# Hybrid decoder layer on eight cores: sums of squares moved from TensorE to POOL, adaLN slots kept between projection pieces, and the last attention head interleaved with the output projection

## The chip, the cores and the metric

The kernel runs on all 8 cores of one Trainium2 chip. Each core computes one of eight sequences, and the cores do not communicate. The metric is the device time of the slowest core, in microseconds (us). Executions of this program have a second, slower state, in which some cores show a lower granted TensorE clock; those executions are left out wherever two kernels are compared. Stage times below are medians over the 8 cores of one profiled execution, so a stage time does not depend on which core happened to be the slowest.

The engines are PE (TensorE), DVE (VectorE), ACT (ScalarE), POOL (GpSimd) and SP (which only issues DMA here).

## The reference, cut to what matters

`x` is (8, 2048, 2048) in float32. The layer is (cut and shortened):

```python
mod = silu(c) @ w_mod + b_mod                  # (B, 6*2048): shift, scale, gate, twice ("adaLN")
h = rmsnorm(x, g_pre_mix) * (1 + sc_a) + sh_a
fq, fk, fv, fg, sq, sk, sv = split(h @ w_in)
fox = forgetting_attention(fq, fk, fv, log_sigmoid(fg + b_forget))   # "FoX": 8 heads, causal, decay bias
swa = sliding_window_sink_attention(rope(sq), rope(sk), sv, sinks)   # 8 heads, window 128
mix = concat(fox, swa) @ w_out
x = x + gt_a * rmsnorm(mix, g_post_mix)
h = rmsnorm(x, g_pre_mlp) * (1 + sc_m) + sh_m
y = square(relu(h @ w_up)) @ w_down            # d_ff = 8192
x = x + gt_m * rmsnorm(y, g_post_mlp)
```

`rmsnorm` needs the sum of squares over the model width for every token. The kernel keeps the width on the 128 partitions and in 16 rows, and 512 tokens along the free axis. A sum over the width is thus a sum over 16 rows and over the partitions.

## The kernel before

The order of the work is: two of the six parts of `mod` with the first projections; FoX heads 0 and 1; sliding window; FoX heads 2 to 7; four tiles of `w_out` (512 tokens each); then up, down, up, down for two halves of the tokens; then a tail with the last residual.

**The filler.** Attention leaves gaps on PE. Between its steps a filler lays pieces of projections for later heads (`main`: 4 matmuls of 128x512 count as 4), and after every 8th piece a *slot* of the other four parts of `mod` (`side`). One slot is four small matmuls on one 1 MB-in-fp32 tile of `w_mod`, which a ring of five buffers loads as 512 KB of bf16.

```python
def _one(self):
    while self.main:
        ...                              # next piece; StopIteration removes it
        self.n += 1
        if self.n % self.every == 0:     # every = 8
            self._side()
        return v
    return self._side()                  # no pieces left: run slots alone

def fill(self, n):
    self.credit += n
    while self.credit > 0:
        v = self._one()
        if v is None:
            self.credit = 0
            return
        self.credit -= v
...
F.main = [q_(1), k_(1), stripe(I_SK, sk_ev(0)), vpair(I_SV, vts)] + [...4 stripes]
fox(0, 64 * 6 + 128 + 64 + 18)           # the second argument is the budget of filling
F.main = [...]
fox(1, 64 * 7 + 128 + 18)
...                                      # sliding window, FoX 2 to 6: 128 + 4 each
F.drain_side()
for m in range(16):
    dma("pool", WO[m](), dram(T["wO"][m]), f"wo{m}")
fox(7, 0, sbanks=[2, 3, 0, 1], la=3)     # last head: nothing to fill with
```

The last slot of each of the four parts is followed by `mod_finish`: DVE copies the result to `stage`, and PE, DVE turn it into a column of `modT`. In the memory layout of before, `stage` shares its 2 KB with `rr`, which every FoX head uses.

**Attention.** A score matmul goes to a bank; DVE subtracts the decay row (`cfb`, loaded by DMA from `crow`), ACT takes the exponential into one of four buffers `Pb`, and PE multiplies `Pb` with V and with ones.

**Sums of squares** after `w_out`, and after `down`, are made on PE: ACT squares each row into a bf16 buffer and PE adds it up over the partitions by a matmul with ones, 16 for one sum.

```python
def stat_add(src, sbk, first, last):
    flush(1)
    q = sqb[cnt["q"] % 2]
    cnt["q"] += 1
    act(q(), src, AF.Square)                       # bf16
    pend.append(lambda: pe([mm(sbk(), ones(), q(), first, last)], ...))

def rstd_of(bk):
    flush(0)
    act(bk(), bk(), AF.Ln, bias=EPS, scale=1.0 / D)
    act(bk(), bk(), AF.Exp, scale=-0.5)
```

While PE computes tile t of `w_out`, the other engines do the two norms of tile t-1 as a list of 35 jobs. Two jobs follow each of the first nine rows and three each of the other seven:

```python
jobs = [lambda: rstd_of(sb1)]                      # norm 1
jobs += [lambda m=m: p1(m) for m in range(KC)]     # y*gate*rstd + x, and its square
jobs += [lambda: rstd_of(sb2)]                     # norm 2 needs all 16 squares of p1
jobs += [lambda m=m: p2(m) for m in range(KC)]     # input of the MLP
if t + 1 < NT:
    jobs += [lambda: x2_load(t + 1)]
```

The softmax here doesn't subtract the row's maximum and nothing guards it: scores larger than these inputs give would overflow.

## Time and profile before

The time before was 3306.3 us (median of 3 runs, 3305.73 to 3306.89).

These lines are from the page of the kernel before: busy time of each engine with its share of the span; three rows of the 40 slices of the span (tenths of busy time, of the full TensorE clock, and of the DMA engines); and the shares of the chain of work that ended last.

```profile
PE 2930.7 (89%) x14392; PEld 1371.9 (41%) x14392; DVE 877.6 (27%) x1343; ACT 754.9 (23%) x1228; POOL 358.5 (11%) x502
...
PE   2278957969888889999999999999999999999994
...
PEclk9988978979999999999999999999999999999997
DMA  9834566460111352336444455555689744444446
...
PE 79%; DMA 7%; DVE 4%; ACT 4%; issue 4%; POOL 2%; DVEq 0%; ACTq 0%; POOLq 0%; SPq 0%
```

The reader should see two things. PE is the limit nearly everywhere, from slice 10 on at 80% or more until the tail. And in slices 6 and 9 (counted from 1) PE falls to 5 and 6 tenths and the clock to 7 tenths, while DMA goes up to 6. The 7% of DMA in the chain must be there.

This is the table of windows for the kernel before: each line is a stretch (start:end, its length), the busy time of each engine, the granted clock, the DMA share and GB/s.

```profile
core 5: us, PE busy (x) PEld busy (x) DVE busy (x) ACT busy (x) POOL busy (x), PEclk, DMA share, GB/s
454.00:509.50 55.50, 13.90 (x95) 5.42 (x93) 3.89 (x8) 2.41 (x4) 11.41 (x20) 0.52 0.94 148
683.00:721.50 38.50, 8.45 (x59) 3.12 (x51) 1.85 (x3) 1.23 (x2) 7.40 (x14) 0.57 1.02 161
721.50:841.00 119.50, 117.30 (x763) 71.13 (x763) 48.60 (x74) 71.83 (x130) 2.11 (x4) 0.98 0.14 25
1156.00:1198.00 42.00, 27.93 (x135) 12.49 (x132) 25.79 (x45) 27.13 (x48) 0.53 (x1) 0.88 0.67 131
1256.40:1470.20 213.80, 192.80 (x865) 83.03 (x863) 131.74 (x192) 96.28 (x156) 0.00 (x0) 0.99 0.31 119
```

The first two stretches, at the ends of FoX 0 and FoX 1, hold 94 us in which PE works 22 us, at about half the clock, and the DMA engines are full. The sliding window (third line) has nearly no DMA (0.14). The fourth line is FoX 7, the fifth is tiles 1 to 3 of `w_out`.

PE's timeline in the first of these stretches shows what PE does there. The columns are start, duration, engine, line, operation, operands, count, and in brackets the idle time before it with what ended that.

```profile
466.71 0.62 PE L379 MATMUL bank<-ring_67,condpad 128*32 128x512 bf16 x4 [4.75 <-DMA ring_67<-w_mod]
470.30 0.62 PE L379 MATMUL bank<-ring_71,condpad 128*32 128x512 bf16 x4 [2.98 <-DMA ring_71<-w_mod]
473.60 0.62 PE L379 MATMUL bank<-ring_68,condpad 128*32 128x512 bf16 x4 [2.69 <-DMA ring_68<-w_mod]
```

Each slot is 0.6 us of work behind 2.7 to 4.8 us of waiting for its tile. Those are the slots that the filler runs when its pieces are used up.

### The profile page before, as it was taken

The numbers are of one execution on the slowest core, as the hardware profiler recorded it, in microseconds if no ns is written. First come the engines' busy times: TensorE is split into PE (matmuls) and PEld (weight loads), VectorE is DVE, ScalarE is ACT, GpSimd is POOL, SyncE is SP. The second block draws the span as 40 slices with busy tenths as digits, with TensorE's granted clock in tenths as the row PEclk, the third lists the DMA queues.
The fourth block names the chain that finished last, engine by engine and source line by source line (L and its number), as shares of the span: only waits on it lengthen the run. The fifth ranks groups of instructions, "written<-read, shape, count | busy, mean of one in ns | idle before, by whom it ended". The sixth has DMA issues, their size and how long they took to land.

```text
span 3307.3 us, 37215 instructions; the slowest of 8 cores (3281.3 to 3307.3 us)
## 1 busy us (share of the span) xinstructions
PE 2930.7 (89%) x14392; PEld 1371.9 (41%) x14392; DVE 877.6 (27%) x1343; ACT 754.9 (23%) x1228; POOL 358.5 (11%) x502
## 2 busy tenths in 40 slices
PE   2278957969888889999999999999999999999994
PEld 0034523436533434334444444444444444444441
DVE  0132323314444445554211100000033311000005
ACT  1141323316445444443211100000111111000000
POOL 1341222210000100000000000000000000000003
PEclk9988978979999999999999999999999999999997
DMA  9834566460111352336444455555689744444446
GB/s 185 154 103 98 87 111 113 85 113 14 29 41 25 61 134 90 115 109 123 76 76 76 77 89 95 92 91 92 127 170 189 143 77 77 77 76 73 75 84 215
DMA packets 99197, 325.71 MB, mean 98 GB/s; under 512 B 12080, under 2 KB 12208, under 8 KB 92624
## 3 DMA queue, kind: packets, MB, share of 16 engines
q0 software_dynamic: 58320, 211.87, 39.4%
q1 hardware_dynamic: 40704, 111.46, 10.0%
q8 instruction: 117, 1.92, 0.2%
q14 instruction: 56, 0.46, 0.1%
HBM read 493.12 MB, written 42.01 MB: 162 GB/s over the span
## 4 chain that ended last, share of the span: by engine, by line
PE 79%; DMA 7%; DVE 4%; ACT 4%; issue 4%; POOL 2%; DVEq 0%; ACTq 0%; POOLq 0%; SPq 0%
PE bank L379 79%; DMA ring_70<-w_mod 5%; DVE bank L399 2%; POOL qrot L399 1%; ACT qrot L396 1%; DMA ring_69<-w_mod 1%; DVE xstA L404 1%; DVE mixF L404 1%; ACT rr L396 1%; ACT sqA L396 1%; DMA xstA<-xP 0%; DMA cfb_83<-crow 0%; ACT Pb_89 L396 0%; DMA cfb_85<-crow 0%; ACT sqb_182 L396 0%
## 5 line engine op out<-in xcount | busy, mean ns | idle before, releaser
L410 DVE TENSOR_SCALAR bank<-bank 128x512 f32<-128x512 f32 x256 | 166.0, 694 | 643.2 <-PE bank L379 643.2
L379 PE MATMUL bank<-mix,rung_110 128*128 128x512 bf16 x1376 | 304.0, 379 | 0.0
L379 PE MATMUL bank<-mix,rung_108 128*128 128x512 bf16 x1376 | 304.0, 379 | 0.0
L379 PE MATMUL bank<-mix,rung_109 128*128 128x512 bf16 x1344 | 296.9, 379 | 0.0
L413 DVE COPY mixF<-bank 128x512 f32<-128x512 f32 x64 | 41.2, 686 | 854.9 <-PE bank L379 854.9
L396 ACT ACTIVATE sqb_181<-bank 128x512 bf16<-128x512 f32 x64 | 38.2, 597 | 890.2 <-DVE mixF L413 852.2
L379 PEld LDWEIGHTS bank<-mix,rung_110 128*128 128x128 bf16 x1376 | 134.7, 98 | 162.3
L379 PEld LDWEIGHTS bank<-mix,rung_108 128*128 128x128 bf16 x1376 | 134.6, 98 | 162.2
L379 PEld LDWEIGHTS bank<-mix,rung_109 128*128 128x128 bf16 x1344 | 131.5, 98 | 158.6
L379 PE MATMUL bank<-hT,ring_68 128*128 128x512 bf16 x640 | 159.7, 384 | 8.8 <-DVE mix L399 5.4
L379 PE MATMUL bank<-hT,ring_69 128*128 128x512 bf16 x512 | 136.2, 406 | 24.4 <-POOL hT L410 16.9
L399 DVE TENSOR_TENSOR bank<-bank,cfb_85 128x512 f32<-128x512 f32 x192 | 117.8, 628 | 119.1 <-PE bank L379 113.6
L399 DVE TENSOR_TENSOR bank<-bank,cfb_83 128x512 f32<-128x512 f32 (+3 forms) x128 | 74.2, 595 | 89.2 <-PE bank L379 77.5
L379 PEld LDWEIGHTS bank<-hT,ring_68 128*128 128x128 bf16 x640 | 61.2, 98 | 79.4 <-issue 16.9
L396 ACT ACTIVATE Pb_87<-bank,Ctok 128x512 bf16<-128x512 f32 x80 | 55.0, 688 | 147.8 <-DVE bank L399 147.7
L379 PEld LDWEIGHTS bank<-hT,ring_69 128*128 128x128 bf16 x512 | 50.3, 103 | 91.0 <-issue 46.7
L379 PE MATMUL bank<-qT_72,kT_73 128*128 128x512 bf16 (+3 forms) x160 | 55.9, 352 | 35.6 <-ACT Pb_87 L396 27.0
L203 POOL DMA_DIRECT2D rung_108<-wU x43 | 22.7, 528 | 584.4 <-PE bank L379 584.4
L399 DVE TENSOR_TENSOR mix<-bank,rr 128x512 bf16<-128x512 f32 x48 | 33.1, 691 | 144.3 <-ACT rr L396 144.3
L396 ACT ACTIVATE Pb_89<-bank,Ctok 128x512 bf16<-128x512 f32 (+1 forms) x80 | 48.2, 602 | 98.5 <-DVE bank L399 98.5
L379 PE MATMUL bank<-qT_74,kT_75 128*128 128x512 bf16 (+3 forms) x160 | 56.8, 360 | 14.5 <-ACT Pb_87 L396 9.1
L379 PE MATMUL bank<-ring_71,hT 128*128 128x256 bf16 x512 | 67.3, 275 | 1.9 <-DVE skT L399 1.9
(672 smaller groups left out, 4547.8 us busy)
## 6 DMA issues: line engine op xcount, KB each, us to landing
rung_108<-wU POOLq DMA_DIRECT2D x43, 512.0 KB, 5.2
rung_110<-wU POOLq DMA_DIRECT2D x43, 512.0 KB, 5.2
rung_109<-wD POOLq DMA_DIRECT2D x43, 512.0 KB, 5.1
rung_108<-wD POOLq DMA_DIRECT2D x43, 512.0 KB, 5.2
rung_109<-wU POOLq DMA_DIRECT2D x42, 512.0 KB, 5.2
rung_110<-wD POOLq DMA_DIRECT2D x42, 512.0 KB, 5.2
outP<-mixF SPq DMA_DIRECT2D x64, 256.0 KB, 3.1
ring_67<-w_mod POOLq DMA_DIRECT2D x25, 512.0 KB, 8.6
```

The source lines that it names most:

```text
L203: return self.op(eng, lambda e: e.dma_start(out=oa, in_=ia), [in_], [out], dsem=dsem, extra=extra)
L379: ins = e.matmul(o, lhsT=l, rhs=rh, start=st, stop=sp)
L396: return P.op("act", lambda e: e.activation(out=out.ap, in_=in_.ap, func=func, **kw), r, [out])
L399: return P.op(eng, lambda e: e.tensor_tensor(out=out.ap, in0=a.ap, in1=b.ap, op=op), [a, b], [out])
L404: return P.op("dve", lambda e: e.scalar_tensor_tensor(out=out.ap, in0=a.ap, scalar=sc, in1=b.ap, op0=op0, op1=op1), r, [out])
L410: return P.op(eng, lambda e: e.tensor_scalar(out=out.ap, in0=a.ap, scalar1=sc, scalar2=None, op0=op), r, [out])
L413: return P.op("dve", lambda e: e.tensor_copy(out=out.ap, in_=a.ap), [a], [out])
```

## The change

The intent has three parts and some support:

1. Slots run only between projection pieces, one per 8 pieces, never alone. They then spread into the sliding window and FoX 2 to 6, where DMA has room. The slots must then not share memory with FoX, so `stage` gets room of its own; that, and most of what follows, is paid for by a smaller scratch area for DMA.
2. FoX 7 is interleaved with the first tile of `w_out`.
3. Squares are kept in fp32 and added row by row on POOL; PE does one fp32 matmul with ones per sum.
4. Support: six `Pb` in place of four, four weight buffers for up/down in place of three, two V pairs swapped in order.

The core of the diff, with cuts:

```diff
-BASE = 16640
+SCRATCH = 4096
+BASE = SCRATCH + 256
+NPB = 6
+NRB = 4
@@ Fill._one
-            return self._side()
+            return None
@@ fox(h, prefill, ..., skip=0, drain=True)
+            w = tot / (n - skip) / 2 if i >= skip else 0
-            F.fill(tot / n / 2)
+            F.fill(w)
             pv(L[i])
@@ order of the heads
-    fox(0, 64 * 6 + 128 + 64 + 18)
+    fox(0, 64 * 7 + 128)
-    fox(1, 64 * 7 + 128 + 18)
+    fox(1, 64 * 7 + 128)
     ... (128 + 4 becomes 128 for the sliding window and FoX 2 to 6)
-    fox(7, 0, sbanks=[2, 3, 0, 1], la=3)
@@ sums
-    def stat_add(src, sbk, first, last):
+    def stat_add(src, acc, first):
+        if first:
+            act(acc(), src, AF.Square)
+            return
         q = sqb[cnt["q"] % 2]
         cnt["q"] += 1
         act(q(), src, AF.Square)
-        pend.append(lambda: pe([mm(sbk(), ones(), q(), first, last)], [ones(), q()], [sbk()]))
+        tt(acc(), acc(), q(), ALU.add, eng="pool")
-    def rstd_of(bk):
-        flush(0)
+    def rstd_of(acc):
+        bk = banks[SBK[cnt["s"] % 3]]
+        cnt["s"] += 1
+        pe([mm(bk(), onesF(), acc(), True, True)], [onesF(), acc()], [bk()])
@@ w_out
+    def out_tile(t, acc, nxt):
+        for m in range(KC):
+            bk = nxt()
+            for q in (0, 2, 3, 1):       # head 7 lies in group 1, so that comes last
+                pe([... 4 matmuls ...])
+                yield 4
+            ... two or three norm jobs, the copy, the square
+    F.every = 1000
+    F.main = [out_tile(0, acc, next_pj)]
+    fox(7, 4 * 34, skip=6, drain=False)
+    x2_load(0, [1, 2, 3])
+    R2.start()
+    F.drain()
@@ memory: sq0, sq1, acc0, acc1 (fp32), stage on its own, ... (cut)
```

## The prediction

> **What bounds it now.** TensorE: the page gives PE 2930.7 of 3307.3 us (89%); in the chain of waits 79% is PE, 7% DMA. A table of windows gives the stages: start and first projections 0-262 us; FoX head 0 to 454; **454-509.5: PE busy 13.9 us, DMA share 0.94, clock 0.52**; FoX 1 to 683; **683-721.5: PE busy 8.5, DMA 1.02, clock 0.57**; sliding window to 841; FoX 2-6 to 1156 (62-66 us each); FoX 7 to 1198; w_out tiles to 1470 (58.4, then 71.3 each); up/down 452, 448, 442, down to 3265; tail 42.
>
> **Change by change.**
>
> 1. *adaLN slots.* The bold windows are slots that the filler runs when its projection pieces are used up: PE's timeline shows 4 small matmuls (0.6 us), then 2-5 us until the next w_mod tile lands, about 3.2 us a slot. The changed filler never does this; 28 slots go, one per 8 pieces, into sliding window and FoX 2-6 (DMA share 0.05-0.25); between pieces one takes 0.34 us. 55.5+38.5 us go, and about 6 us at low clock after them; back come 28x0.34, 3 us of drain, and 3 us at the start of FoX 1 (FoX 3 waits 3.25 there). **-83 us.**
>
> 2. *FoX 7 with tile 0.* PE needs 23 us (FoX) + 55.2 (256 matmuls at 0.2157 start to start); now they take 100.4. About 10 us of early waits (cfb rows late among the w_out loads: 2.9 and 5.0) stay, as the first six steps get no filling. **-10 us.**
>
> 3. *Sums of squares.* 192 ones-matmuls go (41.4 us), with PE's 0.7 us waits for sqb. Added: 180 POOL adds of 1.26 us (the qrot multiply, same shape) and 12 fp32 ones-matmuls: "FP8 and Floating Point Precision" of the Trainium skill says true FP32 takes 4 passes, so I estimate 0.9 us.
>  Tiles 1-3: PE needs 55.2+1.8, but the second fp32 matmul stands right behind the last residual add. DVE (two rows of 1.6 us and a 0.78 copy per 3.45 us of PE) is behind by then; a square (0.63) and an add (1.26) follow: PE waits about 8 us. 65 instead of 71.3: **-17 us**. POOL, 3.8 us per 3.45 there, is nearly as late.
>  Up/down: 80 ones-matmuls less, 4 fp32 more, one longer wait: **-14 us**.
>  Tail: four squares pass through POOL in turn, then two fp32 matmuls: **+4 us**.
>  The skill ("GPSIMD Engine Reference", Key points) says POOL contends with DVE operations with two SBUF inputs. This trace agrees: the mixF+aX add takes 1.76 us beside POOL, 0.69 alone. DVE operations beside the new adds have a PSUM operand, so I expect no slowing.
>
> 4. *Fourth weight buffer, six Pb, layout, V pairs swapped.* PE doesn't wait for weights in up/down (busy 100%): **about 0**.
>
> Sum about -124: **3182 us**, range 3152 to 3214. Faster by over 2%: 0.96; within: 0.03; slower: 0.01.
>
> **What would show it.** No stretch near 455-510 and 680-720 with DMA near 1.0 and clock near 0.5; FoX 2-6 1-2 us longer each; FoX 7 + tile 0 about 90 us; tiles 1-3 about 65 each, with one PE wait of 6-10 us at the fp32 matmul on POOL's accumulator; down 435-437; tail 46; POOL busy 225 us more.
>
> **What would make it wrong.** w_mod loads colliding with weight loads at their new places; w_out loads late for FoX 7; POOL's queue holding back squares and banks (tiles over 70 us); dearer fp32 matmuls; a lower granted clock in the denser program.

## The result, and the profile after

The changed kernel took 3195.69 us (median of 4 runs: 3196.94, 3194.45, 3192.54 and one slow, 3336.93); the kernel before took 3306.02 us beside it. The ratio of fast runs is 0.9663 (95% interval 0.9644 to 0.9682). A ratio here is the mean time of one kernel's fast runs over that of the other's of the same rounds, so it is not quite the ratio of the quoted medians. So the change is faster by 3.4%, about 110 us; the prediction was 124 us.

The same lines of the page, after:

```profile
PE 2873.5 (90%) x13961; PEld 1359.6 (43%) x14224; DVE 876.0 (27%) x1344; ACT 757.9 (24%) x1228; POOL 585.2 (18%) x682
...
PE   2278988998888898999999999999999999999994
...
PEclk8578999999999998999999999999999999999997
DMA  9834545522333833354444455555688644444455
...
PE 79%; DVE 5%; issue 5%; DMA 4%; ACT 4%; POOL 3%; DVEq 0%; POOLq 0%; ACTq 0%; SPq 0%
```

The two dips are gone: from slice 5 on PE is at 8 or more tenths until the tail, and DMA is spread out. POOL is busy 226.7 us longer (585.2 - 358.5). The DMA share of the chain falls from 7% to 4%.

The windows after are FoX 1, sliding window, FoX 7 with tile 0, and tiles 1 to 3. The columns are those of before.

```profile
core 0: us, PE busy (x) PEld busy (x) DVE busy (x) ACT busy (x) POOL busy (x), PEclk, DMA share, GB/s
458.90:629.10 170.20, 159.35 (x904) 82.31 (x916) 60.46 (x96) 54.61 (x92) 38.86 (x45) 0.98 0.47 81
629.10:743.70 114.60, 112.75 (x790) 74.33 (x793) 50.10 (x75) 72.33 (x131) 6.33 (x12) 1.00 0.32 56
1072.60:1162.20 89.60, 83.53 (x386) 38.11 (x394) 36.78 (x61) 37.39 (x63) 19.84 (x18) 0.92 0.72 141
1162.20:1364.70 202.50, 178.36 (x765) 79.25 (x780) 130.02 (x192) 98.28 (x156) 112.56 (x90) 0.93 0.33 125
```

FoX 1 now has a mean clock of 0.98 (only its first microseconds are still at half clock). Tiles 1 to 3 take 202.5 us instead of 213.8, but their clock has fallen from 0.99 to 0.93: something makes PE idle long enough to lose its clock. The timeline around the second sum of tile 1's norms shows it, first the other engines and then PE:

```profile
1197.49 0.69 DVE L404 TENSOR_TENSOR Y_108<-bank,Y_109 128x512 f32<-128x512 f32 x1
1198.26 0.60 ACT L401 ACTIVATE sq_186<-bank 128x512 f32<-128x512 f32 x1 [0.59 <-DVE Y_108 L404]
1200.01 0.63 ACT L401 ACTIVATE sq_185<-Y_108 128x512 f32<-128x512 f32 x1 [1.15 <-POOL acc_188 L404]
1200.78 1.26 POOL L404 TENSOR_TENSOR acc_188<-acc_188,sq_185 128x512 f32<-128x512 f32 x1
...
1190.93 3.62 PE L384 MATMUL bank<-mix,WO_59 128*128 128x512 bf16 x16
1202.19 2.04 PE L384 MATMUL bank<-acc_188,onesF 128*128 128x512 f32 x2 [7.64 <-POOL acc_188 L404]
1204.03 4.79 PE L384 MATMUL bank<-mix,WO_60 128*128 128x512 bf16 x15
...
1232.83 1.02 PE L384 MATMUL bank<-acc_187,onesF 128*128 128x512 f32 x2
1233.69 3.62 PE L384 MATMUL bank<-mix,WO_52 128*128 128x512 bf16 x16
...
1269.36 2.05 PE L384 MATMUL bank<-acc_188,onesF 128*128 128x512 f32 x2 [7.88 <-POOL acc_188 L404]
1433.25 2.04 PE L384 MATMUL bank<-acc_188,onesF 128*128 128x512 f32 x2 [5.13 <-POOL acc_188 L404]
```

DVE's last residual add of the tile ends at 1198.2, 3.6 us after PE has run out of work (1190.93 + 3.62). Its square comes 1.8 us later: ACT first squares another row (0.60 us), and then waits 1.15 us for a buffer that POOL still reads. POOL's add ends at 1202.04. Then the fp32 matmul takes twice as long as the one at 1232.83, which had no wait, and the next row of 16 matmuls takes 4.79 us for 15 of them instead of 3.62 us for 16.

The stages, in us (medians over the 8 cores of one profiled execution):

| stage | before | after | difference |
|---|---|---|---|
| start and first projections | 271.1 | 269.7 | -1.4 |
| FoX 0 | 232.0 | 184.6 | -47.4 |
| FoX 1 | 209.8 | 169.9 | -39.9 |
| sliding window | 119.4 | 114.6 | -4.8 |
| FoX 2 to 6 (sum) | 314.2 | 327.8 | +13.6 |
| FoX 7 and tile 0 | 100.2 | 88.3 | -11.9 |
| tiles 1 to 3 (sum) | 213.9 | 201.4 | -12.5 |
| up, down, up, down, with the last sums | 1792.8 | 1786.0 | -6.8 |
| tail | 45.8 | 44.5 | -1.3 |
| span, median core | 3300.0 | 3187.0 | -113.0 |

### The profile page after: what moved, and what is told of

It is laid out like the page before. It is cut to its first block, busy times and chain, and to the rows that moved or that the text cites. A ratio compares the mean times of both kernels' runs of the same rounds, so it can differ in the third digit from the quotient of the medians.

```text
span 3195.4 us, 36955 instructions; the slowest of 8 cores (3178.6 to 3195.4 us)
## 1 busy us (share of the span) xinstructions
PE 2873.5 (90%) x13961; PEld 1359.6 (43%) x14224; DVE 876.0 (27%) x1344; ACT 757.9 (24%) x1228; POOL 585.2 (18%) x682
## 3 DMA queue, kind: packets, MB, share of 16 engines
q0 software_dynamic: 58320, 211.87, 39.9%
## 4 chain that ended last, share of the span: by engine, by line
PE 79%; DVE 5%; issue 5%; DMA 4%; ACT 4%; POOL 3%; DVEq 0%; POOLq 0%; ACTq 0%; SPq 0%
PE bank L384 79%; DMA ring_70<-w_mod 4%; DVE bank L404 2%; POOL qrot L404 1%; ACT qrot L401 1%; POOL acc_188 L404 1%; DVE bank L409 1%; DVE xstA L409 1%; ACT rr L401 1%; ACT sqA L401 1%; DVE mixF L409 1%; DMA cfb_80<-crow 0%; DMA xstA<-xP 0%; POOL hT L415 0%; DVE mix L404 0%
## 5 line engine op out<-in xcount | busy, mean ns | idle before, releaser
L401 ACT ACTIVATE sq_185<-bank 128x512 f32<-128x512 f32 x59 | 35.2, 597 | 827.5 <-DVE mixF L418 792.9
L384 PE MATMUL bank<-hT,ring_71 128*128 128x512 bf16 x566 | 142.7, 382 | 3.1 <-DVE mix L404 2.2
L384 PE MATMUL bank<-hT,ring_69 128*128 128x512 bf16 x436 | 117.5, 406 | 27.7 <-POOL hT L415 17.4
L404 POOL TENSOR_TENSOR acc_187<-acc_187,sq_185 128x512 f32<-128x512 f32 x59 | 74.7, 1266 | 122.4 <-ACT sq_185 L401 122.4
L384 PE MATMUL bank<-hT,ring_68 128*128 128x512 bf16 x312 | 79.0, 388 | 4.3 <-DVE mix L404 3.1
L404 POOL TENSOR_TENSOR acc_188<-acc_188,sq_186 128x512 f32<-128x512 f32 x59 | 74.4, 1262 | 45.2 <-ACT sq_186 L401 43.0
L384 PEld LDWEIGHTS bank<-hT,ring_71 128*128 128x128 bf16 x576 | 54.9, 98 | 63.2 <-issue 7.4
L384 PE MATMUL bank<-qT_72,kT_73 128*128 128x512 bf16 (+3 forms) x151 | 52.7, 349 | 32.3 <-ACT Pb_87 L401 20.0
L384 PEld LDWEIGHTS bank<-hT,ring_69 128*128 128x128 bf16 x448 | 43.9, 102 | 85.4 <-issue 46.6
L404 POOL TENSOR_TENSOR qrot<-qrot,sinT 128x512 f32<-128x512 f32 x40 | 50.4, 1260 | 128.1 <-ACT qrot L401 128.1
```

Source lines behind the costliest of these rows:

```text
L384: ins = e.matmul(o, lhsT=l, rhs=rh, start=st, stop=sp)
L401: return P.op("act", lambda e: e.activation(out=out.ap, in_=in_.ap, func=func, **kw), r, [out])
L404: return P.op(eng, lambda e: e.tensor_tensor(out=out.ap, in0=a.ap, in1=b.ap, op=op), [a, b], [out])
```

## The experiments

My theory after the result: each part earns what the stage table shows at its place, and the tiles fall short because PE waits for the slow row of engines before the second fp32 matmul and then runs at a low clock. The rivals: the interleaving is not what shortens FoX 7 with tile 0; the supporting parts (six `Pb`) are not free; POOL itself, and not DVE's order of jobs, makes the wait.

All runs give the right result unless the text says otherwise. All ratios are to the kernel before, in the same rounds.

### e1: the slots alone

The kernel before, with only the filler's change, the budgets, and the room that it needs.

```diff
-            return self._side()
+            return None
-    fox(0, 64 * 6 + 128 + 64 + 18)
+    fox(0, 64 * 7 + 128)
 ... (other budgets as in the change; scratch area and own room for stage)
```

> The kernel before with only the filler's change (slots only between projection pieces), and the 2 KB that this needs so that the slot's staging tile no longer lies on another tile. Theory (the slots that ran in a row waited for one w_mod tile each, about 3.2 us): FoX 0 falls from 232 to about 185 us and FoX 1 from 210 to about 170, sliding window to FoX 6 grow by 8 to 15 us together, the whole is about 3306 - 79 = 3227 us (3220 to 3236). Rival (the gain of those two stages comes in part from the six Pb buffers, the swapped V pairs or the new layout, which this kernel doesn't have): over 3240 us, and the sliding window stays at 119 us instead of 115.

Measured: ratio 0.9763 (0.9743 to 0.9782), span of the median core 3222.8, that is -77.2. FoX 0 and 1 take 185.0 and 170.2, together 86.6 less than before, as in the full change. FoX 2 to 6 take 328.7, which is 14.5 more. So the slots are worth about 77 us of the 113. Two things did not move as the theory had it. The sliding window stayed at 120.4, so its 4.8 us in the full change come from something else (see e4). And FoX 7 with tile 0 fell to 95.9 although nothing is interleaved in this kernel (see e2).

### e2: the change without the interleaving

```diff
-    F.every = 1000
-    F.main = [out_tile(0, acc, next_pj)]
-    fox(7, 4 * 34, skip=6, drain=False)
+    fox(7, 0, sbanks=[2, 3, 0, 1], la=3)
     x2_load(0, [1, 2, 3])
     R2.start()
-    F.drain()
+    for _ in out_tile(0, acc, next_ob):
+        pass
```

> The changed kernel with FoX 7 run alone and tile 0 of w_out after it, as before. Theory (tile 0's matmuls fill waits of FoX 7): FoX 7 and tile 0 together take 98 to 101 us instead of 88.4, all other stages stay within 1 us, total about 3207 us. Rival (those 12 us came from the sums leaving PE, not from the interleaving): about 91 us and a total under 3200.

Measured: ratio 0.9665 (0.9646 to 0.9684), and FoX 7 with tile 0 took 91.9, not the 98 to 101 that I expected. My theory missed. The interleaving is worth 91.9 - 88.3 = 3.6 us in its stage and nothing that the total shows (the ratio of the full change is 0.9663).

Where the rest of the 11.9 us came from is seen in PE's waits over this stage. The columns are what waited for what, total us, times, longest. First before:

```profile
PE bank L379 <- ACT rr L396: 9.6, 3, 5.0
PE bank L379 <- ACT Pb_87 L396: 2.9, 1, 2.9
PE bank L379 <- ACT Pb_90 L396: 1.6, 2, 0.8
```

Then e2:

```profile
PE bank L384 <- ACT rr L401: 5.8, 3, 2.1
PE bank L384 <- ACT Pb L401: 3.0, 3, 1.4
```

The waits fell from 14.1 to 8.8 us without interleaving. The ones-matmuls of tile 0 are gone too, 3.1 us by e3. 5.3 and 3.1 make 8.4, and the stage fell by 100.2 - 91.9 = 8.3. The wait that went is named by the kernel before, where the 5.01 us of PE (second line) stand behind ACT, ACT behind DVE, and DVE behind a DMA:

```profile
1165.03 1.90 DVE L399 TENSOR_TENSOR bank<-bank,cfb_85 128x512 f32<-128x512 f32 x3 [5.19 <-DMA cfb_85<-crow]
1168.34 0.59 PE L379 MATMUL bank<-Pb_87,vX 128*128 128x512 bf16 x1 [5.01 <-ACT rr L396]
```

DVE waited 5.2 us in this stage for a `cfb` row before, 2.1 in e2, 1.0 in e3, and not at all in e1 and in the changed kernel. My reading is that the slots now end shortly before FoX 7, so that FoX 7 starts later against the `w_out` loads in front of the `cfb` row; e6, whose slots were all done much earlier, has 1.4 us of this wait again. But this is not shown: e2 (2.1 us) and e3 (1.0) have their slots where the change has them, which has none of this wait, and no run changes the order of these loads alone.

### e3: the change with the sums on PE

`stat_add` and `rstd_of` as before (bf16 squares, 16 ones-matmuls per sum), all else as after. The diff is cut.

```diff
-        tt(acc(), acc(), q(), ALU.add, eng="pool")
+        pend.append(lambda: pe([mm(acc(), ones(), q(), first, last)], [ones(), q()], [acc()]))
-        pe([mm(bk(), onesF(), acc(), True, True)], [onesF(), acc()], [bk()])
+        flush(0)
```

> The changed kernel with the sums of squares back on PE, one bf16 ones-matmul per row, everything else kept. Theory: tiles 1 to 3 go back from 66-68 to about 71 us each (+12 to 13 in all), tile 0 with FoX 7 grows by about 3.5 us (16 ones-matmuls of 0.2157), down 0 by 6.5; up and tail change by under 2 us each; total about 3196 + 22 = 3218 us (3210 to 3225). Rival (moving sums gains little, as the wait at the fp32 matmul gives back what it saves): under 3205.

Measured: ratio 0.9727 (0.9704 to 0.9751), about 20 us slower than the change. Against the change, tiles 1 to 3 take 213.7 (+12.3), FoX 7 with tile 0 91.4 (+3.1), down 448.5 and 451.0 (+6.5, +2.3), the first up 452.2 (+0.6), the second up 442.5 (-1.2), the tail 45.8 (+1.3). The theory held: this part earns its time in the tiles, in down and in tile 0. PE's waits in the tiles before were many and short; these are the two lines for the kernel before, tiles 1 to 3:

```profile
PE bank L379 <- ACT sqb_181 L396: 11.0, 15, 1.1
PE bank L379 <- ACT sqb_182 L396: 10.0, 15, 1.0
```

After, three long waits stand in their place, and their sum is not smaller:

```profile
PE bank L384 <- POOL acc_188 L404: 23.1, 3, 7.9
```

So 21.0 us of waits became 23.1 us. The gain is the removed matmuls, and part of it went to the clock: the short waits did not lower it (0.99), the long ones did (0.93).

### e4: the change with four `Pb` and three weight buffers

```diff
-NPB = 6
-NRB = 4
+NPB = 4
+NRB = 3
```

> The changed kernel with three weight buffers for up and down and four Pb, as before. Theory (neither was waited for): within 4 us of the changed kernel, 3192 to 3200, up and down unchanged within 0.5 us. Rival (six Pb shorten the sliding window, whose exponentials wait for the previous block's products with four): sliding window 118 to 121 us instead of 114.7, total 3199 to 3203; or six Pb lengthen FoX 3 and 6: these go back to 62-64 us and the total is under 3190.

Measured: ratio 0.9676 (0.9657 to 0.9695), which the total can't tell from the change's 0.9663; the stages can. Up and down did not move (450.8, 442.0, 443.7 and 449.0 against 451.6, 442.0, 443.7 and 448.7 with four weight buffers), so the fourth weight buffer is worth nothing here. But the sliding window takes 120.4 instead of 114.6: six `Pb` are worth 5.8 us there. FoX 5 was 2.1 longer and FoX 6 1.7 shorter, about even. My "about 0" was wrong for the `Pb`.

ACT's waits in the sliding window show the cause. In e4:

```profile
ACT Pb L401 <- PE bank L384: 37.4, 31, 1.8
```

In the changed kernel, with six:

```profile
ACT Pb_91 L401 <- PE bank L384: 0.6, 1, 0.6
ACT Pb_89 L401 <- PE bank L384: 0.4, 1, 0.4
ACT Pb_87 L401 <- PE bank L384: 0.3, 1, 0.3
```

With four, about every second exponential (31 of 64) waits until PE has read an old buffer, and the next scores then wait for ACT to leave their bank. On PE this shows as short holds before the score matmuls. Measured from the start times of neighbouring matmuls, beyond what the earlier one takes elsewhere in the stage, there are 54 holds of about 0.13 us with four, 7.7 us in all, and with six only 2, 1.8 us in all. The difference, 5.9 us, is the gain. PE's busy figure does not show them: in the window of before it is 117.30 of 119.50 us. The Trainium skill, "Perfetto Trace Analysis", section "Identifying the Most-Contended Engine", says that matmul busy time is not a good measure of how near PE is to its limit; this trace agrees, as 98% busy hid 5.8 us. The section "Optimization Strategy" of that page says that a bubble that repeats can be a sign of too few buffers, and that is what this was.

### e5: the second fp32 matmul four jobs later

Four empty jobs are put before the second sum, so that two more rows of PE work lie in front of its matmul. The loads of the next tile, before the last job, are now issued in quarters from inside `p2`.

```diff
-        jobs += [r2] + [lambda m=m: p2(m) for m in range(KC)]
-        if t + 1 < NT:
-            jobs += [lambda: x2_load(t + 1)]
+        jobs += [lambda: None] * 4 + [r2] + [lambda m=m: p2(m) for m in range(KC)]
@@ in p2
+            if m % 4 == 3 and t + 1 < NT:
+                x2_load(t + 1, [m // 4])
```

> The changed kernel with the second fp32 ones-matmul of a tile (sum of the residual rows) put two w_out rows later in TensorE's order, the scaling of the second half packed into the last six rows, and the next tile's x loaded in quarters as its room comes free. Theory (PE waits there only because DVE and then the square and the POOL add are later than PE; nothing downstream is short of time): the 7.6 us waits shrink to about 1 us, the low clock after them goes, tiles 1 to 3 fall from 66-68 to about 58 us each, the first up stage by about 5, total about 3196 - 32 = 3164 us (3158 to 3172). Rival (DVE's or POOL's work sets the length of these tiles, the wait only shows it): tiles stay over 64 us, new waits for banks or for x appear, total over 3185.

Measured: 3155.72 us, ratio 0.9548 (0.9528 to 0.9569), a little better than the 3158 to 3172 that I expected. The tiles take 57.9, 58.2 and 57.9, and the first up 443.7 instead of 451.6. In PE's timeline the second matmuls of the three tiles now read:

```profile
1198.10 1.10 PE L384 MATMUL bank<-acc,onesF 128*128 128x512 f32 x2 [0.73 <-POOL acc L404]
1256.34 1.10 PE L384 MATMUL bank<-acc,onesF 128*128 128x512 f32 x2 [1.03 <-POOL acc L404]
1314.26 1.10 PE L384 MATMUL bank<-acc,onesF 128*128 128x512 f32 x2 [0.70 <-POOL acc L404]
```

The waits fell by 6.9 us a tile, and the tiles by 8.4 to 9.8 us. What is more than the wait is the clock: the pair of fp32 records takes 1.10 instead of 2.04 us, and the row behind it is not slowed. 256 matmuls at 0.2157 us and two fp32 ones at 0.86 us are 56.9 us, so at 58 the tile is nearly pure PE work. The edit also moves the loads of the next tile, but these were not what PE waited for: in the change, PE's only waits in tiles 1 to 3 are the three for POOL (23.1 us) and 0.2 us of issue. This settles that the wait, and the clock after it, were the shortfall of the tiles, but for the 1 us between 58 and 56.9. The gain in the total is about 36 us (0.9656 - 0.9548 of 3306 us).

### e6: the slots packed into FoX 3

This puts the slots that are left after FoX 1 into FoX 3, one after every piece, to see what they cost where they are not spread.

```diff
+    F.every = 1000          # from the sliding window on
     for h in range(3, 7):
+        F.every = 1 if h == 3 else 1000
```

> The changed kernel with the 28 adaLN slots after FoX 1 all in FoX 3, one after each of its 32 projection pieces, none elsewhere. Theory (a slot costs PE 0.34 us as long as its w_mod tile has landed, but tiles land only every 3.2 us, so slots closer than that wait): FoX 3 takes 100 to 110 us instead of 66, the sliding window and FoX 2, 4, 5, 6 lose 8 to 14 us together, total 3218 to 3232. Rival (what made the slots dear before was that they ran with no other work between them, not their rate): FoX 3 about 76 us, total about 3190.

Measured: ratio 0.9751 (0.9734 to 0.9769). FoX 3 took 100.1 instead of 66.1. The sliding window, FoX 4 and FoX 6 became 3.1, 2.4 and 4.9 shorter, and FoX 7 with tile 0 2.8 longer. PE's waits in FoX 3:

```profile
PE bank L384 <- DMA ring<-w_mod: 22.1, 17, 3.4
```

The old wait is back, with 17 waits and 22.1 us, now inside a head. So what matters is the density of the slots against the time that a tile needs to arrive, not whether projection pieces run beside them.

### e7: a lighter POOL (wrong result)

For tiles 1 to 3, POOL adds only 64 of 512 columns for all rows of `w_out` but the last. Its adds for the residual rows are left as they were. The sums are wrong, and so is the output (relative error 0.71).

```diff
-        tt(acc(), acc(), q(), ALU.add, eng="pool")
+        sl = slice(0, n)                # n = 64 for these rows
+        tt(acc(sl), acc(sl), q(sl), ALU.add, eng="pool")
```

> The changed kernel with the POOL adds of the w_out rows of tiles 1 to 3 cut to 64 of 512 columns, but for each tile's last row (wrong sums on purpose). POOL then has two full adds per row in the first half of a tile instead of three. Theory (DVE's lateness of 3.6 us, then a square and an add, 2 us, make most of the wait at the second fp32 matmul; POOL's queue adds under 2 us): the wait falls from 7.6 to 5.5-6 us, tiles by 1.5 to 2.5 us each. Rival (POOL, busy without a pause there, sets it): the wait falls below 3.5 us and the tiles by 4 us or more.

Measured: ratio 0.9642 (0.9625 to 0.966). The tiles became 0.7, 2.2 and 2.8 us shorter, and the waits before the second matmul went from 7.64, 7.88 and 7.61 to 6.31, 6.26 and 6.02 us, the first of which reads:

```profile
1197.60 2.04 PE L384 MATMUL bank<-acc,onesF 128*128 128x512 f32 x2 [6.31 <-POOL acc L404]
```

The profile puts the wait down to POOL, as it ended last. POOL had three full adds per row in the first half of a tile and now has two and an eighth, and that removes only 1.3 to 1.6 us of the wait, a little less than I expected. DVE's last residual add still ends 3.6 us after PE has run out of work (1194.9 after 1191.3 in this trace). What got shorter is the step from there to the square, 0.5 us instead of 1.8. The other 2.2 us, the square, the add and the steps between them, are the same in both.

### e8: tile 0 filled in from the first step of FoX 7

Rows 0 and 1 of tile 0 are started with the groups that do not need FoX heads 4 to 7, and filling begins with the first step.

```diff
+        if t == 0:                      # rows 0 and 1: groups 0, 2, 3 first, group 1 later
+            for m in (0, 1):
+                early[m] = nxt()
+                for q in (0, 2, 3):
+                    piece(m, q, early[m])
+                    yield 4
-    fox(7, 4 * 34, skip=6, drain=False)
+    fox(7, 4 * 48, drain=False)
```

> The changed kernel with FoX 7 filled from its first step: the six pieces of the first two w_out rows that don't read head 7 come first, and 48 of the 64 pieces are laid into FoX 7. Theory (the 10 us that FoX 7 and tile 0 take beyond TensorE's 78 are its unfilled first steps and the low clock after them): 80 to 84 us instead of 88.3, total 3187 to 3193. Rival (the waits are for the w_out tiles, which land one every 3 us, or for DVE and ScalarE): 87 us or more, no gain.

Measured: ratio of fast runs 0.9651 (0.9631 to 0.9672). FoX 7 with tile 0 took 86.6, not the 80 to 84 that I expected: another miss. PE's waits in this stage are only 4.5 us on its slowest core. The granted clock in the first 10 us of the stage is 0.66 on seven cores, which I estimate at 3.4 us of lost time (10 us at two thirds of the clock). With PE's 78.2 us of work that makes about 86. Core 0 supports this: its clock there is 0.83, half of that loss, and its stage takes 85.2 us instead of 86.6 to 86.7. The clock falls within 2 us of the start of FoX 7, in a stretch of 5.4 us in which PE works little: it waits 2.19 us for DVE's copy of the last slots' result, and 1.68 us for the first exponential (core 3). That these waits lower the clock, and that filling can't reach them, is my reading; no run removes them.

### e9 and e10: e5 and e8 together, and the change again

> Both edits together: the second fp32 matmul of a tile two rows later, and FoX 7 filled from its first step. The stages they touch don't overlap, so their gains should add: 36 us of the first and 2 us of the second on the median core; FoX 7 with tile 0 at 85 to 87 us, tiles 1 to 3 at 58, first up stage at 444; total 3150 to 3157 us, 4.5 to 4.8% under the kernel before. If the second edit only moves its wait elsewhere, the total is that of the late matmul alone, 3156, or more.

> The changed kernel again, unedited, on the same chip as the run with both edits: 3192 to 3198 us, ratio to the kernel before 0.966; the run with both edits is 1.1 to 1.3% faster than it.

Measured in the same rounds: e9 3155.1 us (3153.38 to 3156.39, 5 runs), ratio 0.9544 (0.9532 to 0.9557); the change again 3192.81 us, ratio 0.9656 (0.9643 to 0.9669). The best kernel is thus 4.6% faster than before and 1.2% faster than the change, but its time is e5's within the spread: the early filling of e8 adds nothing that the total shows, though the median core's span is 3148.2 against 3151.3.

## Why the prediction was right or wrong

The time was inside the range (3195.69, range 3152 to 3214) and the direction right. It was 14 us too low, and the sum came out so near partly because of errors that cancel.

1. **Slots: predicted -83, measured -77 (e1's span).** The mechanism was right: the two long stretches of full DMA and half clock are gone. But the sum is nearer than its terms. For FoX 0 and FoX 1 the prediction had 97 us (55.5, 38.5 and 6 of low clock, less 3 that come back); e1 has 86.6. For what comes back from the sliding window to FoX 6 it had 12.5 (9.5 for the slots at their new places, 3 of drain); e1 has 15.5. (The two make -84.5, which the prediction has as -83.) The span hides half of these two misses by luck, as FoX 7 with tile 0 fell by 4.3 and the first stage by 2.3 in the same execution. The term that was mis-sized most is "55.5 us go". The stretch at the end of FoX 0 was not slots alone: it began with `mod_finish`, for which PE waits for DVE, and this wait stands at the end of FoX 0 in both kernels. These are PE's waits for it in the stretch of before (454 to 509.5; the longest is 4.0 us), and the one wait after:

```profile
PE bank L379 <- DVE modT L399: 4.5, 2, 4.0
458.59 0.40 PE L384 MATMUL bank<-ring_67,condpad 128*32 128x512 bf16 x4 [3.76 <-DVE modT L404]
```

   From the matmuls of `mod_finish` to the start of FoX 1, 54.7 us passed before and 5.3 after, so that 49 went and not 55.5. Most of the low clock at the start of FoX 1 stayed too: over its first 8 us it is 0.56 before and 0.62 after (all medians over the cores).

2. **FoX 7 with tile 0: predicted -10, measured -11.9, for other reasons.** The failed step is "About 10 us of early waits (cfb rows late among the w_out loads: 2.9 and 5.0) stay", and with it that the interleaving earns the 10 us. The early waits mostly went: with part 1 alone the stage is 4.3 us shorter and DVE waits for no `cfb` row (e1; why is open, see e2). The removed ones-matmuls gave 3.1 us (e3), and the interleaving 3.6 us (e2). That the number came out nearly right is luck; it stood on a wrong cause, and only e1 and e2 could show it.

3. **Sums of squares: predicted -17 in the tiles, -14 in up/down, +4 in the tail; measured -12.5, -6.8 and -1.3.** The wait was predicted at "about 8 us" and measured at 7.6 to 7.9. What failed is the step from the wait to "65 instead of 71.3": I added the wait to PE's work at full clock. The tiles took 66.3 to 67.7, since after the wait the fp32 matmul pair took 2.04 instead of 1.02 us and the next row was slow as well. The Trainium skill, "TensorE: Matmul & The Clock Gate", section "What's actually happening", says that the clock falls to half after an idle window of about 3.4 us. This agrees: after 7.6 us the pair takes twice as long, and after the 0.7 to 1.0 us waits of e5 it does not (1.10 us). I had this page at hand and did not use it for that step. 

   For up, down and the tail together I had -14 + 4 = -10; the stage table has -8.1 and e3 9.5, so the net was nearly right. The figure that I gave for it was not: "down 435-437" lies below what 2048 matmuls of 0.2157 us need, 441.8 us, which I could have worked out from the trace. The first down now takes 442.0, so there is no more to get. Nor is the end 4 us longer: the second down, which by this table's marks includes the last two sums, and the tail went from 496.8 to 493.2. PE waits 3.0 us there for POOL against 1.0 us for squares before, but the 32 ones-matmuls that went from the second down (32 x 0.2157 = 6.9 us) outweigh that.

   Two parts of this step held. A 128x512 fp32 matmul takes 0.86 us from its start to the next matmul's (1232.83 to 1233.69), four times 0.2157, as the skill's "FP8 and Floating Point Precision", section "TensorE Precision Notes", has it with four passes. And DVE was not slowed by the POOL adds beside it: its three operations with a PSUM operand keep 751, 692 and 687 ns (750, 692 and 690 before). The skill's "GPSIMD Engine Reference", section "Key points", names only DVE operations with two SBUF inputs, or in a 2-port mode, as contending; that agrees, as the one DVE add with two SBUF inputs takes 1.76 us beside POOL and 0.69 alone. POOL's extra busy time was 226.7 us, predicted 225.

4. **Support: predicted 0, measured -5.8 in the sliding window (e1 and e4).** The failed step is that I looked only at PE's busy share and at the weight waits of up/down. Six `Pb` remove a repeated hold that the busy share hides. The half about the fourth weight buffer was right.

The parts add up. By the span of the median core, e1 gives 77.2 us for the slots (with the 4.3 us at FoX 7 and the 2.3 of the first stage), e3 24.3 for the sums (3211.3 - 3187.0), e4 6.3 for the buffers (3193.3 - 3187.0) and e2 5.3 for the interleaving (3192.3 - 3187.0). Their sum is 113.1, and the change has 113.0. That they meet so closely is luck to some us, as each is one execution; the total times of e2 and the change do not differ clearly. Against this stand the predicted 83, 27, 0 and 10. These make 120: the "about -124" of the prediction left the +4 of the tail out of its sum. Added up rightly it would have been 3186, a little nearer.

## What to carry to other kernels

Work that only fills gaps should never run alone behind its loads: cap its density to what the DMA brings, and spread it into stages that load little; here that was 77 of 113 us. When a reduction moves off PE, put its last step well behind the last operation that feeds it: one wait of 8 us cost more than its length here, since PE also loses its clock, and four empty jobs won about 36 us, a third of what the whole change did. And a PE that is 98% busy can still lose 5% of a stage to a buffer count; ask what the engine that feeds it waits for.

## What the Trainium skill lacked or had wrong

- "TensorE: Matmul & The Clock Gate", section "Back-to-back issue gap", gives about 131 ns per matmul of 512 columns as what a real kernel sustains, and about 216 ns (N/2.4 + 2.5) only for an isolated one. Here the first down of the changed kernel, a stream of weight loads and matmuls that waits for nothing, takes 442.0 us for 2048 matmuls, 215.8 ns each. Other sections of the same page have 215.7 ns for matmuls back to back, and these agree.
- The same page, section "Seeing it yourself", says that with three or more cores of a die in dense matmuls the clock goes to 13/16. In the fast runs here all eight cores run dense matmuls, and the granted clock of the changed kernel reads 1.00 on every core in four windows of 280 to 420 us in up and down. e10's two slow runs have means of 0.80 to 0.82 on cores 4 to 7.
- The same page and "FP8 and Floating Point Precision" give no duration for an fp32 matmul of 512 columns. The runs show 0.86 us at full clock and 1.84 us after a long wait (1202.19 to 1204.03), recorded as two instructions.
- "GPSIMD Engine Reference", section "Performance versus the Vector engine", has a measured fp32 add for 2048 columns only (4497 ns), beside some 2.6 cycles per element. Here 128x512 takes 1.26 us.
- "Perfetto Trace Analysis", section "Identifying the Most-Contended Engine", points to weight-load busy time as a better measure. In the sliding window that was 71.13 of 119.50 us before (60%) and 74.33 of 114.60 after (65%). It leaves room in both, but does not tell where: the 0.13 us holds were seen in start times, and their cause in ACT's waits for its output buffers.
